# A decoder layer on one core: pair 0's V on SyncE's queue, the k halves split from PSUM, and a fourth raw block of output weights in another buffer

## The chip, the core and the metric

The kernel runs on one core of a Trainium2 chip. The metric is the device time of one execution in microseconds (us); lower is better. The engines of a core have queues of their own and work in parallel: PE (TensorE, the matmuls), DVE (VectorE), ACT (ScalarE), POOL (GpSimd) and SP (SyncE, which here issues DMA transfers only). Each engine takes its instructions strictly in order; an instruction that waits for another engine or for a transfer holds everything behind it on its own engine. DMA transfers are issued by an engine (here by SP and by POOL) and land some microseconds later.

## The reference, cut to what matters

One decoder layer on a sequence of 1024 positions with 1024 channels, all in float32: a LayerNorm of the input, then a combined input projection for two groups of heads, whose outputs are concatenated, projected by `w_o`, added to the residual and normalised, and then a gated MLP (2816 channels, with a causal convolution of width 3 before the gate), a residual and another LayerNorm.

```python
def block(args):                       # FoX attention, 8 heads of 64, blocks of 128 queries
    q_i, c_i, i = args
    s = jnp.einsum('bhqd,bhkd->bhqk', q_i, kf) + c_i[..., :, None] - c[..., None, :]
    s = jnp.where(key_pos[None, :] <= q_pos[:, None], s, -jnp.inf)
    p = jax.nn.softmax(s, axis=-1)
    return jnp.einsum('bhqk,bhkd->bhqd', p, vf)
...
# HGRN2, 4 heads of 128, chunks of 64: gated linear recurrence
state = jnp.exp(b_last[..., 0, :])[..., None] * state \
    + jnp.einsum('bhsd,bhse->bhde', k_i * jnp.exp(b_last - b_i), v_i)
```

## The kernel before, in words

**Precision.** Each float32 operand of a matmul is split into a high part (a cast to the fp32r format) and a low part (the operand less its high part), and a product is three matmuls: high by high, low by high, high by low. So every weight tile and most intermediate tiles pass through a cast, nearly always on ACT, and a subtraction on DVE or POOL. For a tile of input weights these are `load_w`: the DMA on SP (L203), the cast (L209) into `whi`, the subtraction (L210) into `wlo`.

**Stages.** In order of time: LayerNorm and the input projections of the recurrent group, the four HGRN2 heads, and from about 325 us the eight FoX heads as four pairs (0 to 3), then the output projection, the MLP and its down projection, and a last LayerNorm. The change lies in the attention stage and in the start of the output projection, from about 325 us to 560 us.

**A pair of heads.** `qk_proj` projects q and then k of a pair, each in two halves of 512 positions (matmuls at L236 into one PSUM bank, `ps3` by the name that the program gives it). For pairs 1 to 3 the result of a half goes through a raw copy: ACT copies it from PSUM to `rq` (L409), which frees the bank; POOL casts `rq` to the high half `qh` or `kh` (L410) and subtracts to get the low half `ql` or `kl` (L411). Pair 0 has no raw copy: ACT writes the high half from PSUM (L413), and DVE takes the low half from PSUM (L414). Then `v_proj` projects V into the same bank, transposes it and splits it into the tile `vst` (cast L449, subtraction L450).

**The filler.** The projections of the pair that follows, and later the first blocks of the output projection, are Python generators. `weighted` calls them as filler between a head's transposes and its weighted sum, so that PE has matmuls to do while a softmax is under way. Tile's scheduler then fixes the order of the instructions on each engine, by a simulation of its own.

**A head.** `head_load` puts a head's operands together by DMAs on SP (L872) from one place in SBUF to another: tiles `q1`, `k1`, `q2`, `k2` of the head, held twice, for even and for odd heads. In the trace those of even heads are `eq`, `eb`, `eg`, `ea` and those of odd heads `q`, `k` and the like, for they reuse earlier buffers; `eb<-kh` is an even head's `k1`, `ea<-kl` its `k2`, and `ea<-qh` an odd head's `q2`. For heads 0 and 1 constant rows come from the DRAM tensor `axd` (L874, L875). `scores` multiplies them (L908), adds the mask (L910), takes the maxima (L913, DVE) and the exponentials (L915, ACT); `normalize` divides (L921, L922); `weighted` transposes the probabilities (L944), splits them (L949 to L955) and multiplies by V (L962), and the two halves of that result are added (L965, L966).

**Pair 0's V.** It is ready before its buffers in the attention stage are free. So `v_proj` writes its two halves to the DRAM tensor `vdr` (L452), and `head_load` of head 0 reads them back into `vst` (L889). Both pairs of DMAs are issued by POOL.

**The first jobs of the output projection.** `early_out` runs inside the attention of the last pair. Job 7 (row block 7, the last 128 positions) uses six of the eight blocks of output weights. A raw block is fetched by `fetch_wo` (L785) and split by `load_wo` (cast L793 on ACT, subtraction L794 on DVE, or on POOL for odd blocks). Blocks 0 and 1 go to `wraw` buffers, blocks 2 and 3 to `wlo` buffers, which the weights of V of pair 3 also use; once a block is split, block +4 is fetched. The job's activations come through `load_rec` (`mr`, L804, and the residual rows `xr`, L808), `load_att` (`ma`, L818) and `load_late` (L826). The matmuls are `o_step` (L841). Two rows of LayerNorm constants, `g1r` and `b1r`, are spread over the partitions by `bcast_row` (L281); they are needed from 618 us on.

Of the kernel before, what the change touches and what calls it, by code (L numbers as in the profile page):

```python
# [9 lines left out]
F32 = mybir.dt.float32  # L10
# [8 lines left out]
P = 128  # L19
S = 1024  # L20
D = 1024
# [102 lines left out]
def body(tc, x, rows, fbias, pp, wi, wt, wo, wup, wdn, cst, msk, out):  # L124
    nc = tc.nc
# [6 lines left out]
    def f(ap):  # L132
        return ap.bitcast(F32)

    top = ExitStack()
    with top:
# [5 lines left out]
        vdr = tc.dram_tile([2, P, S], F32, name="vdr")  # L142
        mixd = tc.dram_tile([2, 8, P, S], F32, name="mixd")
        a1d = tc.dram_tile([NT, P, D], F32, name="a1d")

        wp = pool(top, "wp", 2, "right")
        cp = pool(top, "cst")
# [30 lines left out]
        crow = cp.tile([P, S], F32R, name="crow", tag="crow")  # L178
# [100 lines left out]
        def bcast_row(pl, r, name, tag=None):  # L279
            t = pl.tile([P, D], F32, name=name, tag=tag or name)  # L280
            nc.sync.dma_start(t, rows[r:r + 1, :].broadcast_to([P, D]))  # L281
            return t
# [18 lines left out]
        with ExitStack() as es:  # L301
# [64 lines left out]
            for i in range(NT):  # L366
# [5 lines left out]
                c = slice(i * P, (i + 1) * P)  # L372
# [24 lines left out]
        def qk_proj(p, o, getps, rawt=None):  # L397

            for nm, src, sca in (("q", wt[p], 0.125), ("k", wt[4 + p], 1.0)):
                w = load_w(src)  # L400
                hi = qkp.tile([P, S], F32R, name=nm + "h", tag=nm + "h")
                lo = qkp.tile([P, S], F32R, name=nm + "l", tag=nm + "l")
                for h in range(2):
                    hs = slice(h * 512, (h + 1) * 512)
                    ps = getps(h)
                    yield from proj_half(w, ps, xhi, xlo, h)
                    if rawt:
                        raw = rawt(h)
                        act(raw, ps, AF.Copy, scale=sca)  # L409
                        cpq(RQH)(hi[:, hs], raw)  # L410
                        subq(RQL)(lo[:, hs], raw, f(hi[:, hs]), ALU.subtract)  # L411
                    else:
                        act(hi[:, hs], ps, AF.Copy, scale=sca)  # L413
                        stt(lo[:, hs], ps, sca, f(hi[:, hs]), ALU.mult, ALU.subtract)  # L414
                o[nm + "h"], o[nm + "l"] = hi, lo
# [3 lines left out]
        def v_proj(p, getps, vtile, vstage, getpt, rawt=None):  # L419
# [12 lines left out]
            for h in range(2):  # L432
# [16 lines left out]
                    nc.scalar.copy(vv[:, :, :, 0:64], pv)  # L449
                    tt(vv[:, :, :, 64:128], pv, f(vv[:, :, :, 0:64]), ALU.subtract)  # L450
                if p == 0:
                    nc.gpsimd.dma_start(vdr[h], f(vs))  # L452
                vres[p].append(vv)
                yield

# [321 lines left out]
        xrs = {}  # L777
        mxs = {}
        late = set()

        raws_wo = {}

        def fetch_wo(ki):
            raw = wp.tile([P, D], F32, name="wraw", tag="wlo" if ki in (2, 3) else "wraw")
            nc.sync.dma_start(raw, wo[KORD[ki]])  # L785
            raws_wo[ki] = raw

# [33 lines left out]
        def load_late(i):  # L821

            c = slice(i * P, (i + 1) * P)
            if "late" not in m3:
                m3["late"] = m3["vp"].tile([P, 4, 2, P], F32R, name="m2", tag="vhl")
            nc.sync.dma_start(f(m3["late"][:, i % 4]), mixd[:, 2, :, c].rearrange("j p c -> p j c"))  # L826
            late.add(i)

        def lhs(i, j, k):
# [13 lines left out]
        with ExitStack() as es:  # L843
# [21 lines left out]
            def head_load(hd_):  # L865
# [19 lines left out]
                if hd_ == 0:  # L885
                    vres[0].clear()
                    for hf in range(2):
                        vs = a2.tile([P, S], F32R, name="vst", tag="vhl")
                        nc.gpsimd.dma_start(f(vs), vdr[hf])  # L889
                        vres[0].append(vs.rearrange("p (t n e) -> p t n e", t=4, n=2))  # L890

            def scores(hd_, m):
# [122 lines left out]
            def early_out():  # L1015
# [4 lines left out]
                for i, ks in JOBS:  # L1020
# [9 lines left out]
                    else:  # L1030
                        load_late(i)
                    if 3 in ks and not gb1:
                        gb1.append(bcast_row(gv, 2, "g1r", "g0"))
                        gb1.append(bcast_row(cp, 3, "b1r", "crow"))
                    for h in range(2):
                        hs = slice(h * 512, (h + 1) * 512)
                        ps = jt()
# [687 lines left out]
```

## Time and profile before

| what | value |
|---|---|
| time, median of 3 runs (lowest, highest) | 1357.31 us (1355.51, 1358.41) |
| the profiled execution: its own time | 1358.22 us |
| its span, first to last instruction | 1356.2 us |
| mean granted TensorE clock in it | 0.981 |
| busy share of PE, DVE, ACT, POOL | 95%, 75%, 46%, 15% |
| DMA, mean over the span | 115 GB/s |

The profiled execution is within the three runs, 0.91 us above their median, and 2.0 us of its time lie outside the span. PE is busy in nearly every slice of the page; its granted clock is at full speed (2.4 GHz) but for a few stretches at 0.50, which is the lower level (1.2 GHz). "Idle before" in a row is how long the engine stood still before that instruction, and the name behind it is what it waited for. The idle time of another engine than PE costs nothing unless PE waits for what it does next.

### The profile page before, as it was taken

The page shows a single profiled execution, that of the slowest core. Times are in us where ns is not written, and L with a number is a line of the kernel's source. Part 1 is how long each engine was busy: PE and PEld are TensorE (multiplying, and loading weights), DVE is VectorE, ACT ScalarE, POOL GpSimd, SP SyncE. Part 2 cuts the span into 40 slices and gives each one's busy share as a digit, 9 for nine tenths or more (in the row PEclk, how much of TensorE's full clock was granted, in tenths as well). Part 3 has the DMA queues.
Part 4 walks back from the last instruction along what each step waited for, and adds up shares of the span by engine and source line. Part 5 has one row for each costly group of instructions (what it writes and reads, how often), then busy time and mean ns, then how long its engine had stood idle before and what let it go on. Part 6 is the DMA issues. An engine that isn't in the chain of part 4 may idle for free.

```text
span 1356.2 us, 17299 instructions
## 1 busy us (share of the span) xinstructions
PE 1290.4 (95%) x6457; PEld 1065.5 (79%) x6457; DVE 1016.6 (75%) x1494; ACT 629.5 (46%) x1006; POOL 207.5 (15%) x260
## 2 busy tenths in 40 slices
PE   6999999899889998899889999999999998999997
PEld 5888878778778887688767888888888886888886
DVE  8749586876637675756987888888888876686798
ACT  4246655654536554543344454445444444333450
POOL 3222223131323232201200000000000000000002
PEclk9999999999889999999989999999999999999999
DMA  8411202043543437532321323322333226854233
GB/s 297 141 32 32 71 23 76 29 116 109 128 89 90 90 90 189 190 105 85 143 93 56 104 106 103 115 74 98 109 110 103 92 108 243 296 206 152 90 109 124
DMA packets 68563, 156.41 MB, mean 115 GB/s; under 512 B 6720, under 2 KB 22080, under 8 KB 68480
## 3 DMA queue, kind: packets, MB, share of 16 engines
q1 hardware_dynamic: 57584, 116.78, 28.4%
q0 software_dynamic: 10896, 38.54, 7.5%
q8 instruction: 51, 0.84, 0.3%
q14 instruction: 32, 0.26, 0.1%
HBM read 99.98 MB, written 41.68 MB: 104 GB/s over the span
## 4 chain that ended last, share of the span: by engine, by line
PE 75%; DVE 13%; DMA 4%; ACT 4%; issue 2%; POOL 1%; SPq 0%; POOLq 0%; DVEq 0%; ACTq 0%
PE cu L1281 18%; PE ca L1281 13%; PE pb L1564 7%; PE ps L1564 6%; PE ps L236 5%; PE pb L220 3%; PE ps L841 3%; PE pb L1228 3%; PE ps L962 2%; PE ps L1608 2%; PE pb L236 2%; DVE e L621 2%; PE pb L908 2%; PE ps L662 2%; PE ps L944 2%
## 5 line engine op out<-in xcount | busy, mean ns | idle before, releaser
L1564 PE MATMUL ps<-dw 128*128 128x512 f32 x396 | 94.1, 398 | 2.3 <-ACT dw L1491 2.1
L1188 ACT CAST w<-wt 128x512 fp32r<-128x512 f32 x88 | 54.7, 622 | 88.3 <-PE ca L1281 63.4
L1564 PE MATMUL pb<-dw 128*128 128x512 f32 x396 | 92.1, 393 | 0.0
L1564 PEld LDWEIGHTS ps<-dw 128*128 128x128 f32 x396 | 75.3, 191 | 20.5 <-ACT dw L1491 2.5
L1564 PEld LDWEIGHTS pb<-dw 128*128 128x128 f32 x396 | 74.3, 188 | 17.0
L1188 ACT CAST w<-wraw 128x512 fp32r<-128x512 f32 x66 | 41.0, 623 | 74.4 <-PE cu L1281 69.8
L210 POOL TENSOR_TENSOR wlo<-wraw,whi 128x1024 fp32r<-128x1024 f32 x20 | 51.9, 2594 | 139.0 <-ACT whi L209 111.2
L1318 DVE SCALAR_TENSOR_TENSOR yu<-cu,ppt,yu 128x1023 f32<-128x1023 f32 (+1 forms) x44 | 56.2, 1277 | 14.9 <-ACT yu L1316 14.8
L1189 DVE TENSOR_TENSOR w<-wt,w 128x512 fp32r<-128x512 f32 x88 | 60.2, 684 | 9.2 <-ACT w L1188 9.1
L1492 DVE TENSOR_TENSOR dw<-k,dw 128x1024 fp32r<-128x1024 f32 (+1 forms) x36 | 40.8, 1133 | 34.9 <-PE pb L1564 21.4
L236 PE MATMUL ps<-xhi,whi 128*128 128x512 f32 x144 | 60.9, 423 | 1.3 <-DVE mo L740 1.3
L1281 PE MATMUL cu<-xs1h,w 128*128 128x512 f32 x176 | 60.4, 403 | 1.1 <-ACT xs1h L1153 1.1
L1318 DVE SCALAR_TENSOR_TENSOR ya<-ca,ppt,ya 128x1023 f32<-128x1023 f32 (+1 forms) x44 | 56.4, 1281 | 6.2 <-ACT ya L1316 5.0
L1491 ACT CAST dw<-ar 128x1024 fp32r<-128x1024 f32 (+1 forms) x36 | 35.2, 977 | 53.7 <-PE pb L1564 23.0
L1281 PE MATMUL ca<-x22h,w 128*128 128x512 f32 x176 | 59.0, 395 | 0.9 <-DVE cu L1343 0.9
L913 DVE TENSOR_REDUCE sml<-pb 128x1 f32<-128x896 f32 (+3 forms) x64 | 47.6, 751 | 16.2 <-PE pb L910 15.9
L1281 PE MATMUL ca<-x12h,w 128*128 128x512 f32 x176 | 58.8, 395 | 0.8 <-DVE w L1189 0.8
L1281 PE MATMUL cu<-xs4h,w 128*128 128x512 f32 x176 | 58.8, 395 | 0.7 <-ACT sv L1340 0.7
L1281 PE MATMUL cu<-xs2h,w 128*128 128x512 f32 x176 | 58.8, 395 | 0.0
L236 PE MATMUL ps<-xlo,whi 128*128 128x512 f32 x144 | 58.5, 406 | 0.0
L236 PE MATMUL ps<-xhi,wlo 128*128 128x512 f32 x144 | 57.8, 402 | 0.0
L220 PE MATMUL pb<-xhi,whi 128*128 128x512 f32 x176 | 57.7, 405 | 0.0
(418 smaller groups left out, 3722.9 us busy)
## 6 DMA issues: line engine op xcount, KB each, us to landing
wraw<-in_wup_dram SPq DMA_DIRECT2D x44, 512.0 KB, 3.6
ar<-hd SPq DMA_DIRECT2D x35, 512.0 KB, 3.7
wraw<-in_wt_dram SPq DMA_DIRECT2D x24, 512.0 KB, 3.7
hd<-sab POOLq DMA_DIRECT2D x22, 512.0 KB, 4.3
k<-in_wdn_dram SPq DMA_DIRECT2D x20, 512.0 KB, 5.1
hd<-ya POOLq DMA_DIRECT2D x11, 512.0 KB, 3.1
xres<-xin POOLq DMA_DIRECT2D x8, 512.0 KB, 4.6
wraw<-in_wo_dram SPq DMA_DIRECT2D x8, 512.0 KB, 5.2
```

What stands on the lines that cost most here:

```text
L210: (nc.gpsimd.tensor_tensor if nlw[0] in PW else tt)(lo[:, ks], raw[:, ks], f(hi[:, ks]), ALU.subtract)
L220: mm(ps[:, h * 512:(h + 1) * 512], lhsT=l[:, k, :], rhs=r[:, k, h * 512:(h + 1) * 512], start=k == 0 and n == 0, stop=k == KT - 1 and n == 2)
L236: last_mm[0] = mm(ps, lhsT=l[:, k, :], rhs=r[:, k, h * 512:(h + 1) * 512], start=k == 0 and n == 0, stop=k == KT - 1 and n == 2)
L841: mm(ps, lhsT=lhs(i, j, k), rhs=r[:, k, hs], start=first and n == 0, stop=last and n == 2)
L913: nc.vector.tensor_reduce(sml[:, 0:1], ps[:, 0:n], AX.X, ALU.max, negate=True)
L1188: nc.scalar.copy(sl[:, 0], w[n])
L1189: tt(sl[:, 1], w[n], f(sl[:, 0]), ALU.subtract)
L1228: last_mm[0] = mm(ps[:, hs], lhsT=lhs(i, j, k), rhs=r[:, k, hs], start=k == KORD[0] and nn == 0, stop=k == KORD[-1] and nn == 2)
L1281: last_mm[0] = mm(ps, lhsT=sl[:, wq, k], rhs=xq[:, k], start=bool(first and k == 0 and q == 0), stop=k == KH - 1 and q == 2, skip_group_ch ...
L1318: stt(y[:, d:], c[:, 0:S - d], cw(2 - d), y[:, d:], ALU.mult, ALU.add)
L1492: last_lo[0] = tt(lo, raw, f(hi), ALU.subtract)
L1564: last_mm[0] = mm(sets[bset][t], lhsT=l[:, z, t * P:(t + 1) * P], rhs=r[:, z], start=bool(first and m + z == 0 and l is ah and r is bh), s ...
```

## The change

Four edits. (1) The write and the read of pair 0's V, four DMAs of 512 KB, are issued by SP in place of POOL. (2) In `qk_proj` the second half of k of pairs 1, 2 and 3 no longer takes the raw copy: ACT casts it from PSUM (L413) and DVE subtracts from PSUM (L414). (3) The raw block 3 of output weights takes a `whi` buffer in place of a `wlo` buffer. (4) The DMAs of `g1r` and `b1r` are put behind the latest `load_late`. Line numbers of the changed kernel are one higher from L781 on, and two higher from L1036 on.

```diff
--- before.py
+++ after.py
@@ -404,7 +404,7 @@
                     hs = slice(h * 512, (h + 1) * 512)
                     ps = getps(h)
                     yield from proj_half(w, ps, xhi, xlo, h)
-                    if rawt:
+                    if rawt and not (nm == "k" and h == 1):
                         raw = rawt(h)
                         act(raw, ps, AF.Copy, scale=sca)
                         cpq(RQH)(hi[:, hs], raw)
@@ -449,7 +449,7 @@
                     nc.scalar.copy(vv[:, :, :, 0:64], pv)
                     tt(vv[:, :, :, 64:128], pv, f(vv[:, :, :, 0:64]), ALU.subtract)
                 if p == 0:
-                    nc.gpsimd.dma_start(vdr[h], f(vs))
+                    nc.sync.dma_start(vdr[h], f(vs))
                 vres[p].append(vv)
                 yield
 
@@ -777,11 +777,12 @@
         xrs = {}
         mxs = {}
         late = set()
+        late_ld = []
 
         raws_wo = {}
 
         def fetch_wo(ki):
-            raw = wp.tile([P, D], F32, name="wraw", tag="wlo" if ki in (2, 3) else "wraw")
+            raw = wp.tile([P, D], F32, name="wraw", tag={2: "wlo", 3: "whi"}.get(ki, "wraw"))
             nc.sync.dma_start(raw, wo[KORD[ki]])
             raws_wo[ki] = raw
 
@@ -823,7 +824,7 @@
             c = slice(i * P, (i + 1) * P)
             if "late" not in m3:
                 m3["late"] = m3["vp"].tile([P, 4, 2, P], F32R, name="m2", tag="vhl")
-            nc.sync.dma_start(f(m3["late"][:, i % 4]), mixd[:, 2, :, c].rearrange("j p c -> p j c"))
+            late_ld.append(nc.sync.dma_start(f(m3["late"][:, i % 4]), mixd[:, 2, :, c].rearrange("j p c -> p j c")).ins)
             late.add(i)
 
         def lhs(i, j, k):
@@ -886,7 +887,7 @@
                     vres[0].clear()
                     for hf in range(2):
                         vs = a2.tile([P, S], F32R, name="vst", tag="vhl")
-                        nc.gpsimd.dma_start(f(vs), vdr[hf])
+                        nc.sync.dma_start(f(vs), vdr[hf])
                         vres[0].append(vs.rearrange("p (t n e) -> p t n e", t=4, n=2))
 
             def scores(hd_, m):
@@ -1030,8 +1031,9 @@
                     else:
                         load_late(i)
                     if 3 in ks and not gb1:
-                        gb1.append(bcast_row(gv, 2, "g1r", "g0"))
-                        gb1.append(bcast_row(cp, 3, "b1r", "crow"))
+                        with tc.issue_after(late_ld[-1]):
+                            gb1.append(bcast_row(gv, 2, "g1r", "g0"))
+                            gb1.append(bcast_row(cp, 3, "b1r", "crow"))
                     for h in range(2):
                         hs = slice(h * 512, (h + 1) * 512)
                         ps = jt()
```

What stands on SP where pair 0's V is written and read: `vdr` is the DRAM tensor, `vst` the tile of V, `k_2689` and `q_2690` operands of head 1. Before:

```order
L203 DMA wraw<-in_wt_dram 128x1024
L875 DMA k_2689<-axd 64x1024
L872 DMA q_2690<-qh 64x1024
L872 DMA q_2690<-ql 64x1024
L872 DMA k_2691<-kh 64x1024 x2
```

And now:

```order
L203 DMA wraw<-in_wt_dram 128x1024
L452 DMA vdr<-vst 128x1024 x2
L890 DMA vst<-vdr 128x1024 x2
L876 DMA k_2689<-axd 64x1024
L873 DMA q_2690<-qh 64x1024
L873 DMA q_2690<-ql 64x1024
L873 DMA k_2691<-kh 64x1024 x2
```

V's four DMAs now stand on SP ahead of head 1's first loads; on POOL, where they stood, they are gone.

What stands on SP where heads 2 and 3 get their operands, behind head 3's first `q_2690` (`eb` and `ea` are head 2's k). Before:

```order
L872 DMA q_2690<-ql 64x1024
L872 DMA ea_2688<-qh 64x1024
L872 DMA ea_2688<-oht 16x1024
L872 DMA k_2689<-oht 16x1024
L203 DMA wraw<-in_wt_dram 128x1024
L872 DMA eb_2685<-kh 64x1024 x2
L872 DMA k_2691<-kh 64x1024
L872 DMA ea_2687<-kl 64x1024
```

And now:

```order
L873 DMA q_2690<-ql 64x1024
L873 DMA eb_2685<-kh 64x1024 x2
L873 DMA ea_2687<-kl 64x1024
L873 DMA ea_2688<-qh 64x1024
L873 DMA k_2691<-kh 64x1024 x2
```

The loads of head 2's k stand ahead of `ea<-qh`, two small loads and a 512 KB load of weights, behind which they stood.

What stands on DVE at the end of pair 2's k projection (`ps_3768` is the PSUM bank of that half; `wlo` belongs to pair 2's V weights). Before:

```order
L922 TENSOR_SCALAR pr<-pr,sml 128x768
L953 TENSOR_TENSOR ptl<-ps_3816,pth 128x256
L966 TENSOR_TENSOR u<-ps_3773,ul 64x256
L913 TENSOR_REDUCE sml<-pb 128x1
L210 TENSOR_TENSOR wlo<-wraw,whi 128x1024
L955 TENSOR_TENSOR ptl<-ps_3816,pth 128x128
```

And now:

```order
L923 TENSOR_SCALAR pr<-pr,sml 128x768
L210 TENSOR_TENSOR wlo<-wraw,whi 128x1024
L954 TENSOR_TENSOR ptl<-ps_3815,pth 128x256
L967 TENSOR_TENSOR u<-ps_3772,ul 64x256
L914 TENSOR_REDUCE sml<-pb 128x1
L414 SCALAR_TENSOR_TENSOR kl<-ps_3768,kh 128x512
```

The weights' subtraction moved ahead of three others, and the new L414 stands behind all four.

## Rows read from the trace of the kernel before

**Rows 1.** The page: the chain that ended last, by engine.

```profile
PE 75%; DVE 13%; DMA 4%; ACT 4%; issue 2%; POOL 1%; SPq 0%; POOLq 0%; DVEq 0%; ACTq 0%
```

**Rows 2.** Waits, PE, 325 to 725 us: us in total, times, longest.

```profile
PE pb L1228 <- ACT pb L1238: 1.8, 1, 1.8
```

**Rows 3.** Timeline, PE: start us, us, engine, line, operation, [idle before <-releaser].

```profile
350.23 0.58 PE L962 MATMUL ps<-pth,vst 128*128 128x256 f32 x1 [2.49 <-DMA vst<-vdr]
...
357.99 0.40 PE L908 MATMUL pb<-k,q 128*128 128x512 f32 x1
...
394.26 0.76 PE L908 MATMUL pb<-eb,eq 128*128 128x512 f32 x1 [4.35 <-DMA eb<-kh]
...
449.60 0.50 PE L236 MATMUL ps<-xhi,whi 128*128 128x512 f32 x1
...
540.58 0.79 PE L841 MATMUL ps<-xhi,mr 128*128 128x512 f32 x1 [5.11 <-DMA mr<-mixd]
...
552.43 0.33 PE L944 MATMUL ps<-ct,pr 128*128 128x128 f32 x1 [3.43 <-DVE vst L450]
```

**Rows 4.** Windows, PE: us, PE busy (instructions), granted clock, DMA share, GB/s.

```profile
350.20:355.60 5.40, 5.37 (x20) 0.50 0.50 118
...
394.30:400.10 5.80, 5.80 (x18) 0.50 0.38 85
...
540.60:543.30 2.70, 2.70 (x9) 0.50 1.12 336
...
553.90:557.10 3.20, 3.20 (x11) 0.50 0.71 283
```

**Rows 5.** Timeline, POOL.

```profile
340.81 0.53 POOL L889 DMA_DIRECT2D vst<-vdr  x1 [0.41 <-DMA vdr<-vst]
...
384.61 1.29 POOL L411 TENSOR_TENSOR kl<-rq,kh 128x512 fp32r<-128x512 f32 x1
...
530.74 2.68 POOL L794 TENSOR_TENSOR xlo<-wraw,xhi 128x1024 fp32r<-128x1024 f32 x1 [6.43 <-ACT xhi L793]
```

**Rows 6.** Timeline, SP.

```profile
386.08 1.13 SPq L872 DMA_DIRECT2D eb<-kh  x2
...
534.42 0.98 SPq L804 DMA_DIRECT2D mr<-mixd  x2
```

**Rows 7.** DMA issues, 340.5 to 342 us: KB each, us to landing.

```profile
vst<-vdr POOLq DMA_DIRECT2D x1, 512.0 KB, 9.4
...
q<-ql SPq DMA_DIRECT2D x1, 256.0 KB, 9.1
```

**Rows 8.** DMA issues, 387.2 to 388 us.

```profile
eb<-kh SPq DMA_DIRECT2D x1, 256.0 KB, 7.5
```

**Rows 9.** Groups, L414: ns min, median, max, first and last start us.

```profile
L414 DVE SCALAR_TENSOR_TENSOR kl<-pb,kh x2: 677/678/680, 297.4 to 303.3; 128x512 fp32r<-128x512 f32 x2
```

**Rows 10.** Timeline, DVE.

```profile
447.84 0.42 DVE L966 TENSOR_TENSOR u<-ps,ul 64x256 f32<-64x256 f32 x1 [0.17 <-ACT ul L965]
...
448.70 0.56 DVE L913 TENSOR_REDUCE sml<-pb 128x1 f32<-128x384 f32 x1 [0.44 <-PE pb L910]
...
449.17 1.22 DVE L210 TENSOR_TENSOR wlo<-wraw,whi 128x1024 fp32r<-128x1024 f32 x1
...
548.42 3.35 DVE L794 TENSOR_TENSOR xlo<-wraw,xhi 128x1024 fp32r<-128x1024 f32 x1
```

**Rows 11.** Timeline, ACT.

```profile
380.92 0.61 ACT L409 ACTIVATE rq<-ps 128x512 f32<-128x512 f32 x1
...
447.71 1.04 ACT L209 CAST whi<-wraw 128x1024 fp32r<-128x1024 f32 x1
```

**Rows 12.** DMA issues, 530 to 549 us.

```profile
mr<-mixd SPq DMA_DIRECT2D x6, 256.0 KB, 6.4
...
wraw<-in_wo_dram SPq DMA_DIRECT2D x3, 512.0 KB, 7.3
...
ma<-mixd SPq DMA_DIRECT2D x6, 128.0 KB, 4.8
```

## The prediction, made before the changed kernel ran

> **What bounds the kernel now.** I read the chain that ended last first: PE holds 75% of it, DVE 13% and DMA 4% [rows 1]. So the time falls only where PE stops standing still, and an instruction taken off ACT, POOL or SP is worth nothing by itself. Next I read what PE waited for from 325 to 725 us. Four waits stand out, and the next one is 1.8 us [rows 2]. In the timeline of PE they are 2.49 us for the read of pair 0's V, 4.35 us for head 2's k, 5.11 us for the `mr` of job 7, and 3.43 us for the last part of V of pair 3 [rows 3]. Last I read the granted clock right behind each: it is 0.50 for 5.4, 5.8, 2.7 and 3.2 us, though PE is busy all through those stretches [rows 4]. Work at 0.50 takes twice as long, so each stretch loses half its length: 2.7, 2.9, 1.35 and 1.6 us. A wait of PE here costs itself and that loss: 5.2, 7.25, 6.5 and 5.0 us, 23.9 us in all. The change aims at all four.
>
> **Part 1, V through SP.** PE waits at 350.23 for the second half of `vst` [rows 3], which POOL issued at 340.81 and which took 9.4 us [rows 5, 7]. At the same time SP issues head 1's first loads; one of them, `q<-ql`, of half the bytes, takes 9.1 us [rows 7]. So V shares its bandwidth with loads that are wanted later. In the new order V's DMAs stand on SP ahead of these loads, so V's bytes come first. That removes 2.49 us and the clock's 2.7. What is late next is head 1: its scores begin at 357.99 [rows 3], and at 352.8 once 5.2 us are gone. Its loads lack no byte that they had before, but they don't come sooner; issued from about 341 to 343 with 9.1 us each, the last lands near 352. That is tight, so I keep 4.5 of the 5.2 us. Bounds: 5.2, and 0 if the wait only moves to head 1. SP loses nothing by the wait that it gains (the read waits for the write): its next load, of `axd`, stood in the queue behind the same write before.
>
> The row shows that V's read was slow while another queue's loads were in flight [rows 7]. The Trainium skill ("DMA: Bandwidth & Descriptors", section "Issuing engines are not separate DMA queues") says that DMAs of SyncE and GpSimd run on the same 16 DMA engines and interleave, so that the choice of the issuing engine saves only issue time. By that rule the move alone gives nothing and the wait goes on to head 1, which would make the whole sum 4.5 us worse; I hold against it that here the order changes too, not the issuer alone. It is the third rival below.
>
> **Part 2, k's second half from PSUM.** PE stands from 389.9 to 394.26 for `eb<-kh` [rows 3]. Before, ACT copied the half out of PSUM at 380.92 [rows 11], but POOL had a weight subtraction in front of the cast, so that its `kl` began only at 384.61 [rows 5], and SP issued `eb` at 386.08 [rows 6], landing 7.5 us after issue [rows 8]. Now ACT's own cast ends near 381.5, and `eb` stands on SP in front of the loads that it stood behind. I put its issue at 382.1, 4.0 us sooner, and, with the two halves 0.6 us apart and the same 7.5 us, its landing at 390.2 against PE's arrival at 389.9. `ea` lands half a microsecond later, and head 2's two products now stand closer together on PE. So a rest of some 0.7 us stays: kept 6.5 of 7.25 us. Bounds: 7.25, and 0 if the loads merely share bandwidth again.
>
> What it costs: DVE gets three instructions of 0.68 us [rows 9]. On DVE they hide under PE's work wherever nothing queues for them. But the PSUM bank is now held until L414 is done, and V's projection of the same pair, next on PE, waits for that bank. In pair 1 I find 0.3 us of it, in pair 3 none. Pair 2 is worse. Before, V's first matmul started at 449.60 with no wait [rows 3]. In the new order the weights' cast on ACT (1.04 us from 447.8) comes first [rows 11], so DVE starts its subtraction at 448.85; behind it stand, by rows of the same stretch, 1.22, 0.42, 0.42 and 0.56 us and then the 0.68 of L414 [rows 9, 10]. That ends at 452.15, less some 0.3 us of overlap between instructions: 451.9. PE waits 2.3 us, and by [rows 4] a wait of that size costs about as much again in clock: 4.5 us lost. Bounds: 0 (if DVE gets to L414 first in fact, because PE is itself earlier or later there) and 5.2, the price of the nearest wait, place 1's.
>
> **Parts 3 and 4, job 7.** The `mr` that PE waited for was issued at 534.42, behind raw block 3, and landed 6.4 us later, while loads of weights and activations at 5 to 7 us each filled the DMA engines [rows 6, 12]. With block 3 in a `whi` buffer its fetch no longer waits for the weights of V of pair 3; by the order it goes out ahead of head 6's k, and job 7's `mr` stands on SP ahead of the last head's q. So the 5.11 us and their clock go. PE then reaches its second stop early. Between the two waits it had 8.4 us of work, of which the first 2.7 at half speed [rows 3, 4], so 7.1 us at full speed: from 535.5 it arrives at 542.6. What is late there? SP now holds, in front of the other raw blocks and `ma`, the `xr` of job 7, whose buffer is free when POOL has done two subtractions of 2.68 us from 530.74 on [rows 5]: 536.1. Behind it come a raw block, `ma`, another raw block and job 7's `ma`, issued near 541 by the pace of [rows 6], landing 4.8 us later [rows 12]: 545.8, a wait of 3 us. The last raw block, issued near 538.5, lands 7.3 us later [rows 12], is cast and subtracted (1.04 and 2.68 us): 549.5, some 1.7 us after PE. With 1.4 us of clock this makes 6.0 us, where 11.5 stood (6.5 and 5.0): kept 5.5. The 3.43 us for L450 came from DVE's subtraction of 3.35 us in front of it [rows 10]; in the new order that pair stands elsewhere and I let it go. Bounds: 2 (everything late by a further 3.5 us) and 10 (only the last 1.5 us of the wait stays). Moving `g1r` and `b1r` takes one 512 KB load out of this burst; I value it inside the 5.5, and they are used only from 618 us.
>
> **Sum.** Gains 4.5 + 6.5 + 5.5 = 16.5; losses 0.3 + 4.5 = 4.8; net 11.7. The profiled execution took 1358.22 us (its span of 1356.2 and 2.0 outside), so 1346.5; it lies 0.9 above the median of the runs, so 1345.6 against them.
>
> **Rivals.**
> - *No new wait in pair 2.* For it: DVE's order there hangs on one weight cast, and PE could be held elsewhere just before. Against it: the order is fixed and L414 stands fifth. Then 1345.6 − 4.8 = 1340.8. Chance 0.12.
> - *V's bytes only change places* (place 1 gives nothing). For it: nothing is taken off the DMA engines. 1345.6 + 4.5 = 1350.1. Chance 0.13.
> - *Job 7 keeps its stalls in another form* (the change doesn't do there what it says): the fetch of block 3 is early, but `ma` and the last raw block, which nothing speeds up, become the wait. Gain 0 at that place: 1345.6 + 5.5 = 1351.1. For it: the DMA queues are full there. Chance 0.10.
> - *Both of the last two, and pair 2 at its full 5.2*: 1345.6 + 10.0 + 0.7 = 1356.3, no change. Chance 0.07.
> - *Slower: SP stands behind job 7's `xr`.* That transfer now waits on SP for POOL's second subtraction, and everything behind it (two raw blocks, job 7's `ma`, the blocks of the next jobs) waits along. At 536.1 it costs what I charged. Every microsecond later costs PE one. The gain of 11.7 is used up when the subtraction ends near 548, and from 550.5 on the kernel is measurably slower; at 552 it would be 1345.6 + 16 = 1361.6. For it: the subtraction hangs on a cast and that on a fetch, a chain through three engines. Against it: block 3's fetch now goes out early, so nothing late is left in that chain. Chance 0.07.
>
> **How the numbers follow.** The forecast's chance is 0.51, with its own range of 1341 to 1350 from the bounds of the single terms. The range to hold 8 in 10 reaches from the first rival to near the fourth: 1338 to 1356. A measurement of this kernel can tell about 0.2%, 2.7 us, from no change; faster means below 1354.6. The forecast and the first three rivals lie there, 0.86, of which I take 0.04 away for waits in the new order that I have not seen: 0.82. Within 0.2%: 0.10. Slower: 0.08.
>
> **What would show it.** In the profile after, PE's waits for `vst<-vdr` and for `eb<-kh` should be gone or below 1 us, with the clock back at full speed behind their places. The first V matmul of pair 2 should stand some 2 us for DVE's `kl` of L414. SP should issue job 7's `mr` ahead of the last head's q, and PE's first job 7 matmul should not wait; a wait for `ma` or for POOL's `xlo` should follow, 3 to 5 us in all. I am wrong if head 1's scores wait for their loads, if L414 is done before PE gets to V, or if SP stands at `xr` past 540.

## The result, and the profile after

The changed kernel took 1346.63 us (median of 5 runs, 1340.39 to 1347.79), the kernel before 1356.76 us (5 runs, 1355.51 to 1358.41). The ratio is 0.9907, 95% interval 0.9887 to 0.9928: 10.1 us less by the medians. The forecast was 1345.6, in a range of 1338 to 1356. The profiled execution of the changed kernel took 1343.76 us, with a span of 1342.0 us and a mean granted clock of 0.987; it is 2.9 us below the median of its runs, and that of before was above the median of its own. So the two profiles lie 14.5 us apart, not 10.1, and the difference has to be cut into stages before it is explained.

What PE waits for in the attention stage of the changed kernel, to set beside the four waits of 2.5 to 5.1 us that stood there before [rows 3] (us in total, times, longest; lines are those of the changed kernel):

```profile
PE ps L963 <- DVE ptl L951: 2.5, 1, 2.5
PE ps L963 <- DVE u L967: 1.6, 3, 0.7
PE ps L963 <- ACT pth L955: 1.4, 1, 1.4
PE ps L236 <- DVE mo L740: 1.3, 1, 1.3
```

By name none of the four old waits is left; a new one of 2.5 us, for `ptl`, leads. The timeline of PE at the places that the prediction spoke of:

```profile
346.31 0.35 PE L963 MATMUL ps<-pth,vst 128*128 128x256 f32 x1 [1.43 <-ACT pth L955]
...
354.07 0.47 PE L909 MATMUL pb<-k,ea 128*128 128x512 f32 x1 [0.53 <-DMA k<-kl]
...
438.68 0.39 PE L963 MATMUL ps<-pth,vst 128*128 128x256 f32 x1 [0.58 <-DVE u L967]
...
439.74 0.50 PE L236 MATMUL ps<-xhi,whi 128*128 128x512 f32 x1 [0.44 <-DVE kl L414]
...
528.40 0.38 PE L963 MATMUL ps<-ptl,vst 128*128 128x256 f32 x1 [2.50 <-DVE ptl L951]
...
538.56 0.47 PE L842 MATMUL ps<-xhi,ma 128*128 128x512 f32 x1 [0.45 <-DMA ma<-mixd]
```

The first row answers to 350.23 of before: at V's place PE now waits 1.43 us. The profile puts it down to ACT, but V's read lands at the same time as ACT's cast ends (346.17); in five of the seven other kernels with V on SP ahead of head 1's loads and k from PSUM the same wait is put down to the read, and in all eight it is 1.1 to 1.7 us. The second is what the prediction feared for head 1, 0.53 us for the last of its loads. The third and fourth are pair 2, where the prediction put 2.3 us. The fifth is new. The last is job 7's `ma`, where 3 us were expected. The granted clock behind them (us, PE busy, clock, DMA share, GB/s):

```profile
345.00:360.00 15.00, 13.06 (x78) 1.00 0.67 146
440.00:460.00 20.00, 19.80 (x121) 1.00 0.67 142
528.90:532.80 3.90, 3.90 (x19) 0.58 1.03 364
```

It stays at 1.00 (2.4 GHz) where V and pair 2 are, and falls towards 0.50 (1.2 GHz) only behind the 2.50 us at 528.40. Before it was 0.50 in all four places [rows 4]. How long it stays low behind a wait is not the same in every profile; the part on why the prediction came out right shows it.

The page's order in time can be read as stages from the first and last starts of a few lines of PE: attention (first score, L908, to the last weighted sum, L962), from there to the first MLP product and the MLP's products up to the last (L1281), the down projection with its gap (to the start of the last L1608), and the end (from there to the end of the span).

| profile | before the first score | attention | MLP | down | end | span |
|---|---|---|---|---|---|---|
| before | 333.5 | 308.2 | 488.9 | 217.7 | 7.9 | 1356.2 |
| after | 332.5 | 294.9 | 487.4 | 216.1 | 11.1 | 1342.0 |
| part 1 alone | 334.3 | 304.4 | 489.3 | 217.7 | 11.1 | 1356.8 |
| part 2 alone | 333.0 | 300.2 | 487.6 | 217.7 | 7.8 | 1346.3 |
| part 3 alone | 332.7 | 300.7 | 487.1 | 216.0 | 8.6 | 1345.1 |
| without part 3 | 335.0 | 300.3 | 491.7 | 217.6 | 11.1 | 1355.7 |
| without part 4 | 332.7 | 295.0 | 487.0 | 216.1 | 11.1 | 1341.9 |
| pair 2 by the raw copy | 333.4 | 293.0 | 490.6 | 217.7 | 11.1 | 1345.8 |
| before, other output DMAs | 335.0 | 307.0 | 487.9 | 217.7 | 8.1 | 1355.7 |
| after, other output DMAs | 334.8 | 293.0 | 487.7 | 217.7 | 11.1 | 1344.3 |
| after, other output DMAs, pair 2 by the raw copy | 334.9 | 292.4 | 491.5 | 217.7 | 11.1 | 1347.6 |

The last four rows are experiments below. The attention stage, in which the edits stand, lost 13.3 us. The first column scatters by 2.5 us among kernels that are alike up to there; that is the noise of one profile. So are the 1.7 us of the down projection: its first wait is 2.08 us before and after, and the granted clock of the 4.4 us behind it is 0.61 before and 1.00 after. The MLP's column is not noise alone. In the first 60 us behind the attention stage the scheduler's order of the instructions differs between the kernels, and in the three of 490.6 us and more PE waits there for a tile for which the changed kernel has no such wait (here without part 3):

```profile
PE cu L1283 <- DVE xs1l L1156: 3.0, 1, 3.0
```

So by way of the scheduler the edits reach further than 560 us, the end that I had given for the change. The end does not scatter: it is 11.1 us in one group and about 8 in the other. More on it below. Attention and end together give 13.3 − 3.2 = 10.1 us. That this is the difference of the medians to the decimal is chance. In the second pair of profiles, before and after with other output DMAs, where the instructions of this stage are the same and in the same order, they give 14.0 − 3.0 = 11.0, beside 10.5 by the medians.

### The profile page after: what moved, and what is told of

Same layout as the page of the kernel before. It is cut to its first block, busy times and chain, and to the rows that moved or that the text cites. A ratio compares the mean times of both kernels' runs of the same rounds, so it can differ in the third digit from the quotient of the medians.

```text
span 1342.0 us, 17311 instructions
## 1 busy us (share of the span) xinstructions
PE 1283.8 (96%) x6457; PEld 1059.3 (79%) x6457; DVE 1016.4 (76%) x1497; ACT 630.1 (47%) x1006; POOL 199.7 (15%) x250
## 4 chain that ended last, share of the span: by engine, by line
PE 60%; DVE 5%; DMA 1%; ACT 1%; issue 1%; POOL 0%; POOLq 0%; DVEq 0%; ACTq 0%
PE cu L1283 18%; PE ca L1283 13%; PE pb L1566 7%; PE ps L1566 6%; PE ps L842 3%; PE ps L236 3%; PE pb L1230 2%; PE ps L1610 2%; PE ps L963 2%; PE ps L945 1%; DMA mixd<-u 1%; PE pb L909 1%; DVE xlo L795 0%; PE ps L976 0%; PE ps L1152 0%
## 5 line engine op out<-in xcount | busy, mean ns | idle before, releaser
L220 PE MATMUL pb<-xhi,wlo 128*128 128x512 f32 x176 | 57.5, 400 | 0.0
```

Source lines behind the costliest of these rows:

```text
L220: mm(ps[:, h * 512:(h + 1) * 512], lhsT=l[:, k, :], rhs=r[:, k, h * 512:(h + 1) * 512], start=k == 0 and n == 0, stop=k == KT - 1 and n == 2)
```

## The experiments

Each ran beside the kernel before on the same chip; "before" is its median there (1357.0 to 1357.1 us, 21 to 31 runs). Ratios are to the kernel before. The changed kernel itself was measured on another occasion, beside a kernel before of 1356.76 us.

### Part 1 alone

```diff
-                    nc.gpsimd.dma_start(vdr[h], f(vs))
+                    nc.sync.dma_start(vdr[h], f(vs))
...
-                        nc.gpsimd.dma_start(f(vs), vdr[hf])
+                        nc.sync.dma_start(f(vs), vdr[hf])
```

> The kernel before with part 1 alone: pair 0's V is written and read through SP's queue. Theory (the four places are separate and their gains add): PE's 2.49 us for V and the stretch at half clock behind it go, head 1's loads leave a wait of about half a microsecond; 3 to 4.5 us faster than before, 1352.5 to 1354. Rival (the bytes only change places, as DMAs of all issuers share the same engines): the wait moves to head 1's loads, less than 1.5 us of difference.

Measured: 1355.78 us, ratio 0.9997 (0.9981 to 1.0013), 12 runs. Neither theory as written: the rival's number came out, but not for its reason, for no wait went to head 1's loads. The attention stage is 3.8 us shorter, a number that the theory gave too, but only 1.9 us of it stand at V's place; the others stand further on, where the part moves nothing. The time is not shorter, since the end is 3.2 us longer. At its place the part gives less than in the changed kernel:

```profile
348.99 0.36 PE L962 MATMUL ps<-pth,vst 128*128 128x256 f32 x1 [2.30 <-DMA vst<-vdr]
```

PE still waits 2.30 us for V there, and the clock falls behind it. The second half of V took 7.0 us to land, against 6.3 in the changed kernel and 9.4 before [rows 7]; in the changed kernel it lands sooner:

```profile
vst<-vdr SPq DMA_DIRECT2D x1, 512.0 KB, 6.3
```

So V's place is won by less than a microsecond of a transfer.

### V's read on SP, but behind head 1's loads

The changed kernel, with the block that reads V issued after head 1's loads:

```diff
-                if hd_ == 0:
+                if hd_ == 1:
                     vres[0].clear()
```

> The changed kernel, with the read of pair 0's V still on SP but behind head 1's loads in place of ahead of them. Theory (what helped is V's place in the order: its bytes go first): V's read is issued some 5 to 6 us later, near 345, and lands near 350 to 351, so PE waits 4 to 5 us for it in head 0 and the clock falls behind that: 6 to 9 us slower than the changed kernel, near the kernel before or up to 3 us faster than it. Rival (it is the queue that counts: SP's in place of POOL's): V's read takes 5 us wherever it stands on SP, PE's wait stays under 2 us, and the time is that of the changed kernel within 3 us.

Measured: 1353.13 us, ratio 0.9969 (0.9953 to 0.9986), 10 runs; attention 302.2 us.

```profile
354.76 0.58 PE L963 MATMUL ps<-pth,vst 128*128 128x256 f32 x1 [4.71 <-DMA vst<-vdr]
```

The wait is 4.71 us, and the stage 7.3 us longer than in the changed kernel. V's reads took 5.6 us here (median of the two), issued when head 1's loads are partly landed. So the order is what helped: SP's queue with V last is worse than POOL's. That agrees with the rule of the Trainium skill that the prediction weighed ("DMA: Bandwidth & Descriptors", "Issuing engines are not separate DMA queues"), by which DMAs of all issuers run on the same engines and interleave: V's read took 9.4 us among head 1's loads, 7.0 and 6.3 ahead of them and 5.6 behind them. A run with POOL issuing V ahead of head 1's loads was not made, so a share of the queue itself is not ruled out. At the end of the program the issuer does matter, as told below.

### Part 2 alone

```diff
-                    if rawt:
+                    if rawt and not (nm == "k" and h == 1):
```

> The kernel before with part 2 alone: the second half of k of pairs 1 to 3 is split from PSUM. Theory (gains add, and pair 2's bank costs little): the 4.35 us for head 2's k and the clock behind it go, 6 to 7.3 us faster, about 1350. Rival of the prediction (the bank held for L414 costs pair 2's V 4.5 us): 2 to 2.5 us faster, about 1354.5, with a wait of V's first matmul of pair 2 for L414 of 2 us and more.

Measured: 1354.13 us, ratio 0.9977 (0.9957 to 0.9997), 12 runs; attention 8.0 us shorter. The wait for head 2's k is gone. What stands at pair 2 and at job 7:

```profile
445.18 0.51 PE L236 MATMUL ps<-xhi,whi 128*128 128x512 f32 x1 [0.44 <-DVE kl L414]
...
536.58 0.79 PE L841 MATMUL ps<-xhi,mr 128*128 128x512 f32 x1 [5.36 <-DMA mr<-mixd]
...
546.45 0.33 PE L944 MATMUL ps<-ct,pr 128*128 128x128 f32 x1 [1.29 <-DVE vst L450]
```

The first row is the rival's wait: 0.44 us, not 2 and more. The last answers to the 3.43 us for L450 before: 1.29 us, though nothing of part 3 is in this kernel; the scheduler's order there came out another way, and 4.2 of the 8.0 us come behind pair 3's projections, at job 7. The medians give 2.9 us of the 8.0 (the interval reaches to 5.8, and the runs spread over 12 us; the profiled execution is 5.7 us below their median); what became of the rest isn't explained.

### Part 3 alone

```diff
-            raw = wp.tile([P, D], F32, name="wraw", tag="wlo" if ki in (2, 3) else "wraw")
+            raw = wp.tile([P, D], F32, name="wraw", tag={2: "wlo", 3: "whi"}.get(ki, "wraw"))
```

> The kernel before with part 3 alone: raw block 3 of the output weights in a buffer of its own, so that it is fetched early; g1r and b1r stand where they stood. Theory: the 5.1 us for mr and the 3.4 us for L450 go with their clock, and in their place DVE's two subtractions of weights meet POOL's two and take 6 us where they took 2.4, with a wait of PE of about 2.5 us for ptl and the clock behind it: 3 to 7 us faster, 1350 to 1354. Rival: part 4 is what clears this place (b1r's 512 KB in the burst), and part 3 alone gives under 2 us.

Measured: 1353.0 us, ratio 0.9974 (0.9959 to 0.9989), 12 runs; attention 7.5 us shorter. The time and the waits are those of the theory: the waits for `mr` and L450 are gone, and these stand there:

```profile
532.94 0.38 PE L962 MATMUL ps<-ptl,vst 128*128 128x256 f32 x1 [2.52 <-DVE ptl L950]
...
543.69 0.47 PE L841 MATMUL ps<-xhi,ma 128*128 128x512 f32 x1 [2.65 <-DMA ma<-mixd]
```

But 2.7 of the 7.5 us are won by pair 1's V, 100 us ahead of the first instruction that stands otherwise than before; they are no work of part 3. The profiled execution is the fastest of the 12, 5.6 us below their median.

### Without part 3

The changed kernel, with the line of part 3 as it was before.

> The changed kernel without part 3 (raw block 3 in a wlo buffer, as before). The attention stage became 3.8 us shorter with part 1 alone, 8.0 with part 2 alone and 7.5 with part 3 alone, 19.3 in all, but 13.3 with all of them. Theory (part 2 alone also clears the wait for L450 at job 7, by moving the order there, so part 3's gain overlaps it): without part 3 the stage is 297 to 299 us, 2 to 4 us longer than with it. Rival (part 3 carries what was predicted for job 7, 5.5 us): 300 us and more.

Measured: 1356.66 us, ratio 1.0001 (0.9984 to 1.0018), 12 runs; attention 300.3 us, 5.4 longer than with part 3. My theory of an overlap falls; the rival holds, by a little. The 19.3 us of the three parts alone were no clean sum: 2.7 of part 3's stand where it does nothing, and 4.2 of part 2's in an order of job 7 that parts 1, 2 and 4 together do not have. Job 7 waits as it did before, 5.42 us for `mr`, and more behind it:

```profile
533.30 0.79 PE L842 MATMUL ps<-xhi,mr 128*128 128x512 f32 x1 [5.42 <-DMA mr<-mixd]
...
544.07 0.47 PE L842 MATMUL ps<-xhi,ma 128*128 128x512 f32 x1 [1.15 <-DMA ma<-mixd]
...
545.80 0.79 PE L842 MATMUL ps<-xlo,ma 128*128 128x512 f32 x1 [1.26 <-DVE xlo L795]
```

Parts 1, 2 and 4 together measure as nothing; part 3 alone gives 4.0 of the 10.1 us by the medians, so the parts do not add. Of the 10 us between this kernel and the changed one, 5.4 stand in the attention stage and 4.3 in the MLP, mostly at its start, in the wait of 3.0 us for `xs1l` and the low clock behind it: an order of the scheduler's that was not planned.

### Without part 4

```diff
-                        with tc.issue_after(late_ld[-1]):
-                            gb1.append(bcast_row(gv, 2, "g1r", "g0"))
-                            gb1.append(bcast_row(cp, 3, "b1r", "crow"))
+                        gb1.append(bcast_row(gv, 2, "g1r", "g0"))
+                        gb1.append(bcast_row(cp, 3, "b1r", "crow"))
```

> The changed kernel without part 4: g1r and b1r are issued in the burst of job 7's loads again. Theory (part 4 is a small part of the gain): job 7's ma and raw blocks land up to 2 us later, PE's wait for ma grows from 0.45 to about 2 us; 0 to 3 us slower than the changed kernel. Rival (part 4 clears the place): 4 us slower and more.

Measured: 1348.75 us, ratio 0.9939 (0.9917 to 0.9961), 7 runs. Attention is 295.0 us, 0.1 longer; PE's wait for `ma` is 0.44 us, as with part 4. The theory's wait of 2 us is not there: in the trace part 4 gives nothing.

### Pair 2 by the raw copy

```diff
-                    if rawt and not (nm == "k" and h == 1):
+                    if rawt and not (nm == "k" and h == 1 and p != 2):
```

> The changed kernel, but pair 2's second half of k takes the raw copy again. Theory (the held bank costs pair 2 what the traces show, 1.3 to 2 us with no loss of clock): PE's waits of 0.58 and 0.44 us at pair 2 go, and the stage from pair 2's k to pair 3's q is 1 to 2 us shorter; the whole is 1 to 2 us faster, which the runs alone hardly tell. Rival (what pair 2 loses is the order on DVE, where the weights' subtraction stands first, not the bank): the 0.58 us stays, only the 0.44 goes, under 1 us.

Measured: 1348.24 us, ratio 0.9931 (0.9904 to 0.9958), 4 runs; attention 293.0 us, 1.9 shorter. Both waits of pair 2 are gone. What the held bank costs can be read between two of ACT's copies from PSUM, that of pair 2's second half of k and that of its second half of V; before, in the changed kernel, and here:

```profile
448.94 0.61 ACT L409 ACTIVATE rq<-ps 128x512 f32<-128x512 f32 x1
...
471.73 0.61 ACT L427 COPY vt<-ps 128x512 f32<-128x512 f32 x1
```

```profile
437.24 0.60 ACT L413 ACTIVATE kh<-ps 128x512 fp32r<-128x512 f32 x1
...
462.62 0.60 ACT L427 COPY vt<-ps 128x512 f32<-128x512 f32 x1
```

```profile
438.25 0.60 ACT L409 ACTIVATE rq<-ps 128x512 f32<-128x512 f32 x1
...
462.21 0.59 ACT L427 COPY vt<-ps 128x512 f32<-128x512 f32 x1
```

That is 22.8, 25.4 and 24.0 us, and each of the other profiles is within 0.1 us of one of the three. So the bank costs 1.4 us, as expected. Another 1.2 us are lost with the raw copy too; the order of the instructions differs there from before, and which of them it is was not isolated. The stage's 293.0 by itself would be no proof: the changed kernel with other output DMAs (below), which is the same in this stage, also came to 293.0. The whole is not faster than the changed kernel, for this one has the wait for `xs1l` at the start of the MLP, which is 3.2 us longer.

### DVE in place of POOL for blocks 1 and 3

```diff
-WOP = range(1, 8, 2)
+WOP = (5, 7)
```

> The changed kernel, with the subtractions of output weight blocks 1 and 3 on DVE in place of POOL (blocks 5 and 7 stay on POOL); the order on DVE is the same but for the four subtractions in a row. Theory (DVE's two subtractions took 5.94 us because POOL's two ran beside them): the four take about 4.8 us on DVE alone, PE's wait of 2.5 us for ptl falls below 1 us and the clock stays up: 2.5 to 4 us faster than the changed kernel, about 1343. Rival (DVE is short of time there whoever subtracts; two more on DVE push ptl later): the wait grows by 2.4 us or more, 2 to 5 us slower than the changed kernel, about 1350.

In the changed kernel DVE's two subtractions of weights, and POOL's two beside them:

```profile
521.02 5.94 DVE L795 TENSOR_TENSOR xlo<-wraw,xhi 128x1024 fp32r<-128x1024 f32 x2 [2.81 <-ACT xhi L794]
```

```profile
520.12 2.41 POOL L795 TENSOR_TENSOR xlo<-wraw,xhi 128x1024 fp32r<-128x1024 f32 x1 [4.53 <-ACT xhi L794]
...
522.96 2.91 POOL L795 TENSOR_TENSOR xlo<-wraw,xhi 128x1024 fp32r<-128x1024 f32 x1 [0.43 <-ACT xhi L794]
```

DVE needs 5.94 us for two, while POOL runs from 520.12 to 525.87. With all four on DVE:

```profile
518.81 4.63 DVE L795 TENSOR_TENSOR xlo<-wraw,xhi 128x1024 fp32r<-128x1024 f32 x4 [1.81 <-ACT xhi L794]
```

4.63 us for four. So the clash is shown, and the theory is right about it: the 2.50 us for `ptl` is gone, and PE is at job 7's `ma` at 532.7 in place of 538.1. But the time, for which the theory said 1343, is 1349.7 us, ratio 0.9943 (0.9922 to 0.9963), 7 runs, no better than the changed kernel, since PE now meets this:

```profile
537.15 0.76 PE L842 MATMUL ps<-xhi,ma 128*128 128x512 f32 x1 [4.41 <-DMA ma<-mixd]
```

Job 7's `ma` goes into a buffer that the transposed V of pair 3 holds, so it isn't issued sooner: SP waits 2.2 us for that buffer. 4.41 us of a new wait for 2.50 of the old.

### And job 7's `ma` in another buffer

```diff
-                ma = m3["ma"].tile([P, 2, 3, P], F32R, name="ma", tag="asq")
+                ma = wp.tile([P, 2, 3, P], F32R, name="ma", tag="wlo")
```

> The changed kernel with the subtractions of blocks 1 and 3 on DVE, as in the run before, and with job 7's ma in a wlo buffer (which part 3 left free) in place of the buffer that the transposed V holds until PE is done with it; ma then stands on SP ahead of the last raw blocks. Theory (with the DVE clash gone, ma's buffer was the next wait, 4.4 us and the clock behind it): the wait for ma goes; the next late thing is raw block 5's split on POOL, 0 to 2.5 us; 3 to 6 us faster than the run with ma where it was, 1344 to 1347 on the chip that gave 1349.7. Rival (the DMA engines are full there, so something lands as late whatever the order): another wait of 3 to 5 us, for xlo or xhi of block 4 or 5, takes its place and the time stays within 2 us.

Measured: 1349.23 us, ratio 0.9943 (0.9920 to 0.9966), 7 runs; attention 297.0. The rival holds. The wait for `ma` is gone, and PE waits for ACT's cast of block 4:

```profile
535.61 0.79 PE L842 MATMUL ps<-xhi,ma 128*128 128x512 f32 x1 [4.39 <-ACT xhi L794]
```

```profile
534.51 1.04 ACT L794 CAST xhi<-wraw 128x1024 fp32r<-128x1024 f32 x1 [4.48 <-DMA wraw<-in_wo_dram]
```

ACT in its turn waited 4.48 us for that block's transfer. The DMA engines' mean busy share is 1.07 from 530 to 535 us. In this burst the transfers are the limit; what was moved ahead made another land late.

### The end of the program

Four more DMAs on SP, by cutting the output DMAs of row blocks 0 and 1 into halves; first in the changed kernel, then in the kernel before:

```diff
-                    nc.sync.dma_start(out[i * P:(i + 1) * P, hs], yf[:, hs])
+                    for q in range(2 if i in SPLIT else 1):
+                        w = 256 if i in SPLIT else 512
+                        qs = slice(h * 512 + q * w, h * 512 + (q + 1) * w)
+                        nc.sync.dma_start(out[i * P:(i + 1) * P, qs], yf[:, qs])
```

> The changed kernel with four more DMAs on SP: the four output DMAs of row blocks 0 and 1 are cut into halves, so that the last output DMA falls on semaphore 6 of SP's eight and not on 2. In the profiles so far the stretch from the start of the last matmul to the span's end is 11.1 us in the six kernels with V on SP (last DMA on semaphore 2) and 7.8 to 8.6 us in the three with V on POOL (last DMA on 6). Theory (the end depends on which of the eight semaphores the last DMA falls on, so part 1's four more DMAs on SP made the end longer): the stretch goes to about 8 us and the time falls by about 3 us against the changed kernel, to 1344. Rival (it is V on SP, or POOL's fewer DMAs, whatever the semaphore): 11.1 us, and no change.

> The kernel before with the same four more output DMAs, so that its last one falls on semaphore 2 and not on 6; V stays on POOL. Theory (semaphore of the last DMA): the end grows from 7.9 to 11.1 us, 3 us slower than before, 1360. Rival (V on SP): 7.9 us, no change.

Measured: 1346.54 us, ratio 0.9939 (0.9918 to 0.9961), 8 runs, with an end of 11.1 us; and 1357.01 us, ratio 1.0012 (0.9991 to 1.0033), 12 runs, with an end of 8.1 us. The theory of the semaphores falls: the last DMA changed its semaphore in both, and the end stayed with the place of V.

### The shortest stage, with those output DMAs

Pair 2 by the raw copy and the four more output DMAs.

> The changed kernel with pair 2's second half of k by the raw copy, and the four more output DMAs: the version with the shortest attention stage so far (293.0 us from the first score to the last weighted sum, against 294.9 of the changed kernel and 308.2 of before) and, if the semaphore theory holds, the short end. Theory: 8 us at the end, 1 to 2 us less in attention, 4 to 5 us faster than the changed kernel, about 1342.5. Rival: the end stays at 11.1 us, 1 to 2 us faster at most, 1345 and above.

Measured: 1350.47 us, ratio 0.9957 (0.9938 to 0.9976), 12 runs; attention 292.4 us, end 11.1 us. On the same chip the changed kernel with these output DMAs alone took 1346.54 us, so with the raw copy at pair 2 it is 3.9 us slower by the medians, though the stage is the shortest: the MLP is 3.8 us longer, with the wait for `xs1l` at its start. No version that was run beats the changed kernel by more than the scatter.

## Why the prediction came out right, and which steps did not

The terms, measured as the time from the first score to ACT's copies that follow each place, and to the last weighted sum. The first pair of profiles is before and after; the second is the same two kernels with other output DMAs, alike in this stage, instruction for instruction:

| term | predicted | first pair | second pair |
|---|---|---|---|
| place 1, V | 4.5 gained | 3.3 | 4.5 |
| place 2, head 2's k | 6.5 gained | 7.2 | 4.7 |
| pair 2 (predicted: with pair 1's 0.3) | 4.8 lost | 2.4 lost | 2.3 lost |
| job 7 | 5.5 gained | 5.2 | 7.1 |
| attention stage | 11.7 gained | 13.3 | 14.0 |
| end of the program | nothing | 3.2 lost | 3.0 lost |

So one pair of profiles gives a single term to about 2 us. One reason is the clock. The prediction priced each wait with the stretch of low clock that followed it in one profile, and that stretch is not the same each time. Behind the 4.35 us of place 2 the clock was 0.50 for 5.8 us [rows 3, 4]; in the kernel before with other output DMAs the wait was 3.00 us and the clock of the 5.8 us behind it 0.71. Behind the 2.50 us for `ptl` the changed kernel's clock was 0.58; with other output DMAs the same wait left it at full speed:

```profile
529.10 0.39 PE L964 MATMUL ps<-ptl,vst 128*128 128x256 f32 x1 [2.52 <-DVE ptl L952]
```

```profile
529.50:533.40 3.90, 3.90 (x25) 1.00 1.06 385
```

**Place 1.** Right in kind. The wait for V was to be gone or below 1 us, and 1.1 to 1.7 us of it stay; what went is the rest and the low clock. Head 1's scores wait 0.53 us for their loads at 354.07, which the prediction had named as a sign of being wrong; in the seven other kernels of this kind that wait is not above 0.4 us. The experiment with V behind shows that the order did it.

**Place 2.** Right: the wait for `eb` is gone in every kernel with part 2 (in two of them 0.5 us for `ea` stays). ACT writes the high half straight from the bank, and SP issues `eb` 1.2 us later; the two issues of `eb` in 1.89 us are followed by PE's scores with no wait that the list shows.

```profile
376.62 0.61 ACT L413 ACTIVATE kh<-ps 128x512 fp32r<-128x512 f32 x1
...
435.50 1.05 ACT L209 CAST whi<-wraw 128x1024 fp32r<-128x1024 f32 x1 [0.94 <-PE ps L236]
```

```profile
377.84 0.58 SPq L873 DMA_DIRECT2D eb<-kh  x1
...
526.43 0.45 SPq L809 DMA_DIRECT2D xr<-xres  x1
```

**Pair 2.** The mechanism was right, the size was not: 1.02 us of waits (0.58 and 0.44) and no loss of clock, where the step said 2.3 us and as much again. Between ACT's two copies (see the experiment with the raw copy) 2.6 us are lost, 1.4 of them by the bank. The prediction's first rival takes off 4.8 us for it, where pair 2's share was 4.5. The step took the cast at 447.71 [rows 11], which it writes as 447.8, for the earliest that it could be. But that cast had stood behind two other instructions on ACT; now that it comes first, it runs when PE is done with the old weights (the second row of ACT above, 0.94 us idle and released by PE). The copy of pair 2's second half of k stands 11.7 us earlier than before (437.24 and 448.94), so in the time of before the cast runs at 447.2, 0.5 us sooner, and L414, which ended at 439.69 (the row below), at 451.4, 0.5 us sooner than the step's 451.9. PE asked for the bank at 439.30, which is 451.0, 1.4 us later than the 449.60 that the step took; 0.58 us of that is the wait for an addition on DVE. So 0.4 us of a wait were left, and the clock stayed at 1.00.

```profile
439.02 0.67 DVE L414 SCALAR_TENSOR_TENSOR kl<-ps,kh 128x512 fp32r<-128x512 f32 x1
```

**Job 7.** The sum of 5.5 was near (5.2 and 7.1), but not what it was made of. The `mr` left the path as predicted. SP did not stand at `xr` at all: POOL's second subtraction ended at 525.87, and SP, issuing one load behind the other, came to `xr` at 526.43 (the last row of SP above), so the rival of a slower kernel did not come about. What was late next was neither `ma` (0.45 us, expected 3) nor the last raw block. It was DVE: with block 3 fetched early, POOL's two subtractions run back to back beside DVE's two, and these last 5.94 us, and the splits of the probabilities stand behind them. I had the sign of this in front of me, a DVE subtraction of 3.35 us [rows 10], beside which POOL ran one of its own (from 548.35 on), and used it only for the wait that went.

**The end.** The prediction costed part 1's move of four DMAs from POOL to SP at nothing outside its place. In 10 profiles with V on SP the end took 11.1 us, in 4 with V on POOL 7.8 to 8.6. So part 1 wins 3.3 to 4.5 us at its place in the whole change, 1.9 alone, and pays 3.2 for it, and alone it measures as nothing. That the oversized pair 2 and this overlooked end nearly cancel is why the forecast of 1345.6 lies so close; that is luck.

Where these 3.2 us stand can be read. The busy share of the DMA engines in the last 8.2 us of the span, in 40 slices, before and after:

```profile
DMA  1000000000000000000000049597795950000000
```

```profile
DMA  0000000197795968900000000000000000000000
```

The output is over 1.4 us before the end of the span in the one, and 4.7 us before it in the other. What the end waits for then is POOL's DRAIN, an instruction at the end of POOL's program that the timeline does not list. Of POOL's three DRAINs at the end the first is the long one (ns shortest, median and longest; first and last start), before and after:

```profile
L1721 POOLq DRAIN  x3: 40/102/1452, 1350.7 to 1355.9; - x3
```

```profile
L1723 POOLq DRAIN  x3: 40/93/7898, 1333.3 to 1341.7; - x3
```

Before, it lasts 1.45 us and is over before the last output has landed. After, it begins at 1333.3 and lasts 7.90 us, past the last output, and the span ends 0.8 us behind it, as in all ten profiles with V on SP. It lasts 7.90 us in all ten and 1.45 to 1.79 us in the four with V on POOL. The number of DMAs on SP does not decide it: the kernel before with other output DMAs issues as many there as the changed kernel. Why POOL's DRAIN takes so long when POOL has issued V's four DMAs less is open; whether it is their number on POOL or V's by themselves wasn't tried.

## What to carry to other kernels

Order the transfers by when they are wanted: V's read ahead of or behind other loads of the same queue moved the stage by 7 us. Which engine issues them is not free either: when DMAs move to another engine, compare the end of the program too. When a wait is removed, list what then runs side by side: two engines that share the work of one split can be slower than one of them alone, and in a burst where the DMA engines are full, the wait that goes can show the next transfer. Don't take the low clock behind a wait from one profile as its fixed price. And cut two profiles into stages before comparing them, those too that the edit does not touch, for the scheduler may order them anew: here a gain of 3.8 us in one stage and a loss of 3.2 at the far end gave a measured difference of nothing.

## What was not expected of the hardware

Moving four 512 KB DMAs from GpSimd to SyncE, a thousand microseconds before the end, went with an end of the program that is 3.2 us longer, in every profile, and with a closing DRAIN of POOL of 7.90 us in place of 1.45 to 1.79. Two subtractions of 128x1024 on DVE took 5.94 us beside POOL's, and four took 4.63 us without them. A wait of PE of 2.5 us was followed by a low clock in one profile, and by none in another of the same instructions. The same attention stage, instruction for instruction, came to 294.9 and 293.0 us in two profiles, so one profile each can't tell steps of 1 to 2 us apart in it.
